# A hybrid attention, long-convolution and expert layer on one Trainium2 core: the Hyena filter network's last layer, taps, decay and transform become steps between the dense pieces

## The chip, the cores and the metric

The kernel runs on one core of a Trainium2 chip. The metric is the device time of one execution in microseconds; before the change it is 1257.59 us (median of 3 runs, 1257.53 to 1258.89).

## The reference

One layer over 256 latent tokens and 256 context tokens, width 1024, all in f32. What matters here:

```python
h = rms_norm(x, norm1_g) * (1 + sc1) + sh1          # sh1, sc1: silu(c) @ ada_w + ada_b
q, k, v, hy, gates = split(h @ w_in + b_in)         # the same for the context rows (k, v used)
oa = diff_out(diff_attention(rope(norm(q)), [k_ctx, rope(k)], [v_ctx, v], lam))
# Hyena branch
hdn = sin(freq * (z @ w1 + b1)); hdn = sin(freq * (hdn @ w2 + b2)); hdn = sin(freq * (hdn @ w3 + b3))
kf  = (hdn @ w4).reshape(L, 2, 512) * exp(-t * deltas)          # taps, decay
ob  = x0 * irfft(rfft(x1 * v) * rfft([k_fwd, 0, k_bwd reversed]))
x  += g1 * ((sig(ga) * (oa @ w_up_a) + sig(gb) * (ob @ w_up_b)) @ w_out)
x  += g2 * moe(modulated rms_norm(x))               # top 4 of 32 experts, clamped SwiGLU
```

The filter network depends on no token: it works on a fixed table of positions (33 x 256) and on its weights.

## The kernel before

**Dense pieces.** The projections are done as 128-row pieces of weight, 512 columns each, in a fixed order: q (first half, pieces 0 to 3), h1 (4 to 7), q again (8 to 11), h1 again (12 to 15), k (16 to 23), v (24 to 31), then hv, h0, the gates and the up projections. h1, hv and h0 are the three Hyena streams. Each weight and each activation is split into a rounded part and a remainder ("hi" and "lo"), and `mm3` does three multiplies with them. A weight's hi part is a ScalarE cast and its lo part a subtract on VectorE or GpSimd (`prep_hi`, `prep_lo`; a list of pieces says whose lo goes to GpSimd); the tile of two pieces is called `wsp`, and three of them rotate.

**Order.** Nothing is reordered by a scheduler: each engine executes its instructions in the order in which the code emits them, and waits where it must. After each piece `piece_done` emits the steps that the table `TASKS` lists for that piece, in the table's order; a step is a generator, and each number in its tuple is a piece after which it goes on to its next `yield`. So a step's place on an engine's queue is fixed by the table, and a step that waits holds everything behind it on that engine.

**Before the first piece** stand the loads, the statistics of x, the modulation vectors (`ada_half`, `mods_half`: the first half of channels before q, the second half between piece 7 and piece 8), the transposes of x (`columns_of`), and, woven in, all three sine layers of the filter network (`filter_layer`, `filter_sin`), the split of its last weight (`filter_weights`, two subtracts on GpSimd) and the taps (`filter_taps`, which hold four PSUM banks). The decay (`filter_decay`: two multiplies on VectorE, a sum and a difference on GpSimd, then a split into `KSD`) is a step after pieces 2 and 6, the split of the transform's matrix (`dft_parts`, subtract on GpSimd into `FG`) after piece 2. The transform (`filter_dft` and `filter_end`: 30 multiplies, tiles `ps_kf` and `ps_kn`, copied to `KF`) stands on TensorE after `mods_half(1)` and ahead of piece 8.

**Memory.** 25 slots of 8 KB per partition hold arrays and loaded weights. `ROOM` bounds the loads held at each count of takes and releases; `done` and `release` free a slot and start the next load in a fixed order (`prefetch`). The DMAs are issued by SyncE.

**Other names.** `q_out` transposes the rotated queries (`ps_qt`) after piece 22 and copies them to `QT` (a ScalarE cast, then a VectorE subtract) after piece 23. `ada` steps accumulate the rest of the modulation vectors on VectorE (`AA`). `ctx_stats`, `ctx_norm`, `ctx_columns`, `ctx_modulate` prepare the context rows (`CT`), which the k pieces need; `ps_c` are their transposes, after piece 14. The experts' weights (400 MB) stream in at the end.

Of the kernel before, what the change touches and what calls it, by code (L numbers as in the profile page):

```python
# [11 lines left out]
F32 = mybir.dt.float32  # L12
F32R = mybir.dt.float32r
# [3 lines left out]
AF = mybir.ActivationFunctionType  # L17
# [3 lines left out]
P = 128  # L21
# [12 lines left out]


TASKS = [
    ("filter_decay", (1,), (2,)), ("dft_parts", (0,), (2,)), ("filter_decay", (0,), (6,)), ("ctx_stats", (), (8,)),
    ("later_loads", (), (11,)), ("ctx_norm", (), (13,)), ("ada", (1, 0), (14,)), ("ctx_columns", (), (14, 17)),
    ("ctx_modulate", (0,), (15,)), ("ctx_modulate", (1,), (15,)), ("q_raw", (0,), (16, 18, 19)), ("ctx_modulate", (2,), (16,)),
    ("q_raw", (1,), (16, 19, 20)), ("tables", (), (16,)), ("vec2_cols", (), (17, 17)), ("hyena", (3, "h1", 4), (18, 20)),  # L40
# [116 lines left out]
def tile_kernel(ctx: ExitStack, tc: tile.TileContext, a: dict, out: bass.AP):  # L157
# [44 lines left out]
    def quarter(shape, dt=F32):  # L202
        return part("RAW", shape, dt)
# [36 lines left out]
    def want(key, shape, src):  # L240
        pending.append((key, shape, src))
# [11 lines left out]
    def then(f):  # L253
        pending.append((None, None, f))
# [17 lines left out]
    want("x", [P, 2, 1024], [(i, a["x"][0, i * P:(i + 1) * P]) for i in range(2)])  # L272
    want_half(0, 0)
    want_half(0, 1)
    then(lambda: sp.dma_start(W4[0:64], a["filt_w4"][0]))
    want_half(0, 2)
    want_half(0, 3)
    want_in("q", 0)
    q0 = w_in[0:512, 0:512].rearrange("(k p) n -> p k n", p=P)
    pending[-1] = (("in", "q", 0), [P, 4, 512], [(slice(k, k + 2), q0[:, k:k + 2]) for k in (0, 2)])  # L280
    want_in("h1", 0)
    then(lambda: filter_loads())
    for kk in range(4):
# [134 lines left out]
    def dft_parts(j):  # L418
        if j:
            FGs[1] = alloc([P, 2, 1024], "FG1", F32R)  # L420
            IDFTs.extend(FGs[1][:, j].rearrange("p (m t) -> p m t", m=4) for j in range(2))
        (gp.tensor_copy if j else act.copy)(FGs[j][:, 0], raw_fg[j])
        gp.tensor_tensor(FGs[j][:, 1], raw_fg[j], FGs[j].bitcast(F32)[:, 0], ALU.subtract)
        return iter(())

    def filter_loads():
        sp.dma_start(DEC, a["k_decay"].rearrange("(i p) c -> p i c", p=P))
        sp.dma_start(KF[:, 0:2], a["k_dft"].rearrange("(i p) c -> p i c", p=P))
# [16 lines left out]
    cT = wk.tile([P, KC, 32], F32, tag="t1", name="cT", bufs=4)  # L445
    dve.memset(cT, 0.0)
    fold = kept([P, NE], "fold")
    FS = wk.tile([P, 2, P], F32R, tag="sq", name="FS")


    B0 = kept([P, 512], "B1")
# [107 lines left out]
    def filter_layer(i):  # L559
        if i == 0:  # L560
            hs[0] = sin_layer(0, [Z[0:33, 256:320]] * 2, [Z[0:33, h * P:(h + 1) * P] for h in range(2)])
        else:
            up = [slice(64 * h, 64 * h + 64) for h in range(2)]
            hs[i] = sin_layer(i, [Z[u, 256 + 64 * i:320 + 64 * i] for u in up], [hs[i - 1][0][u] for u in up])

    def filter_sin(i):
        h, ar = hs[i]
        if i < 2:
            act.activation(h, ar, AF.Sin)
            return  # L570

        hi = wk.tile([P, P], F32R, tag="hz", name="fhi", bufs=3)
        act.activation(h, ar, AF.Sin)
        act.activation(hi, ar, AF.Sin)
        for j in range(2):
            u = slice(64 * j, 64 * j + 64)
            dve.tensor_tensor(FS[64:128, j], h[u], hi.bitcast(F32)[u], ALU.subtract)
            act.copy(FS[0:64, j], hi[u])

    def filter_weights():  # L580
        act.copy(WS[0:64, 0], W4[0:64])
        act.copy(WS[64:128, 0], W4[0:64])
# [3 lines left out]
    taps = []

    def filter_taps():
        for i in range(2):
            for d in range(2):  # L590
                ps = pst(f"ps_k{i}{d}", True)
                for j in range(2):
                    pe.matmul(ps, FS[:, i], WS[:, j, d * 512:(d + 1) * 512], start=(j == 0), stop=(j == 1))
                taps.append(ps)
        release("WS")

    def filter_decay(i):
        kw = []
        for d in range(2):
            kt = quarter([P, 512], F32)  # L600
            dve.tensor_tensor(kt, taps[2 * i + d], DEC[:, i], ALU.mult)
            unhold(f"ps_k{i}{d}")
            kw.append(kt)
        if i == 0:
            dve.memset(kw[1][0:1, :], 0.0)
        ks = quarter([P, 512], F32)
        gp.tensor_tensor(ks, kw[0], kw[1], ALU.add)
        gp.tensor_tensor(kw[1], kw[0], kw[1], ALU.subtract)
        for d, v in enumerate((ks, kw[1])):
# [12 lines left out]
    def filter_end():
        ps = pst("ps_kn")
# [111 lines left out]
    filter_weights()
    columns_of(X0, XT, "x", (0,))
    filter_sin(1)
    spin(SPINS[3])
    filter_layer(2)
    ada_half(0, 1)  # L740
    more_columns()
    ada_half(0, 2)
    columns_of(X0, XT, "x", (1,))
    done("x")
    filter_sin(2)
    prep_hi(0)
    spin(SPINS[4])
    ada_half(0, 3)
    mods_half(0)
    filter_taps()  # L750
    for k in range(4):
        modulate_split(XT, XTs, 0, dve, (k,))
        if k == 0:
# [132 lines left out]
    def filter_decays(i):
        filter_decay(i)
        return iter(())

    steps.update(dft_parts=dft_parts, filter_decay=filter_decays, later_loads=later_loads, ada=ada_step, release=release, tables=tables, lambda_=lambda_, hyena=hyena)  # L890
# [889 lines left out]
```

## Time and profile before

| | |
|---|---|
| median of 3 runs | 1257.59 us |
| the profiled execution | 1257.4 us, its span 1255.7 us |
| TensorE busy, weight loads | 88%, 42% |
| VectorE busy | 41% of the span |
| ScalarE, GpSimd busy | 22%, 13% |
| DMA | 467.10 MB, mean 372 GB/s |
| mean granted TensorE clock | 0.982 |

The times of the rows below are microseconds from the span's start; the profiled execution is 1.7 us longer than its span. An idle time in brackets says how long the engine had stood still before the instruction, and what ended it. The kernel has two parts: some 320 us up to the routing, and the experts.

### The profile page before, as it was taken

The page shows a single profiled execution, that of the slowest core. Times are in us where ns is not written, and L with a number is a line of the kernel's source. Part 1 is how long each engine was busy: PE and PEld are TensorE (multiplying, and loading weights), DVE is VectorE, ACT ScalarE, POOL GpSimd, SP SyncE. Part 2 cuts the span into 40 slices and gives each one's busy share as a digit, 9 for nine tenths or more (in the row PEclk, how much of TensorE's full clock was granted, in tenths as well). Part 3 has the DMA queues.
Part 4 walks back from the last instruction along what each step waited for, and adds up shares of the span by engine and source line. Part 5 has one row for each costly group of instructions (what it writes and reads, how often), then busy time and mean ns, then how long its engine had stood idle before and what let it go on. Part 6 is the DMA issues. An engine that isn't in the chain of part 4 may idle for free.

```text
span 1255.7 us, 14038 instructions
## 1 busy us (share of the span) xinstructions
PE 1104.1 (88%) x5547; PEld 532.6 (42%) x5547; DVE 511.1 (41%) x808; ACT 276.7 (22%) x503; POOL 168.6 (13%) x152
## 2 busy tenths in 40 slices
PE   7889789998999899897798879887988797888896
PEld 5678678897433433332242233223322332232222
DVE  5699996967222323331232223123212322223222
ACT  6563464654210111110010011001000100011110
POOL 2386455323000000000000000000000000000000
PEclk9999898999999999999999999999999999999998
DMA  9984534978899999999999999999999999999994
GB/s 335 400 313 148 175 134 191 347 293 358 334 412 417 417 417 417 418 417 418 417 416 417 417 417 417 417 417 417 418 418 418 417 417 418 417 418 417 417 416 177
DMA packets 98450, 467.10 MB, mean 372 GB/s; under 512 B 8800, under 2 KB 9804, under 8 KB 63564
## 3 DMA queue, kind: packets, MB, share of 16 engines
q1 hardware_dynamic: 95056, 462.26, 91.4%
q10 hardware_dynamic: 3324, 3.88, 1.0%
q8 instruction: 46, 0.75, 0.2%
q14 instruction: 24, 0.20, 0.0%
HBM read 465.07 MB, written 1.05 MB: 371 GB/s over the span
## 4 chain that ended last, share of the span: by engine, by line
DMA 54%; PE 28%; DVE 11%; ACT 2%; issue 2%; POOL 1%; ACTq 0%; SPq 0%; DVEq 0%; POOLq 0%
PE ps_eg L1497 6%; PE ps_eu L1497 6%; PE ps_ey L1529 5%; DMA w___w___10__3__4181<-in_exp_w_dram 2%; DMA w____w___18___0__5264<-in_exp_w_dram 2%; DMA w___w___28__7__6440<-in_exp_w_dram 2%; DMA w___w___20__3__5389<-in_exp_w_dram 2%; DMA w___w___11__7__4343<-in_exp_w_dram 2%; DMA w___w___22__3__5666<-in_exp_w_dram 2%; DMA w___w___14__3__4676<-in_exp_w_dram 2%; DMA w___w___24__3__5884<-in_exp_w_dram 2%; DMA w___w___18__3__5171<-in_exp_w_dram 2%; DMA w___w___26__3__6161<-in_exp_w_dram 2%; DMA w___w___27__7__6323<-in_exp_w_dram 2%; DMA w___w___23__7__5828<-in_exp_w_dram 2%
## 5 line engine op out<-in xcount | busy, mean ns | idle before, releaser
L1541 DVE TENSOR_TENSOR yr<-ps_ey,G 64x512 f32<-64x512 f32 x62 | 42.7, 688 | 387.2 <-PE ps_ey L1529 386.6
L479 POOL CAST pick<-both 128x128 fp32r<-128x128 f32 x32 | 24.6, 770 | 842.4 <-PE ps_eu L1380 842.3
L1542 ACT ACTIVATE YS<-yr,wsl 64x512 fp32r<-64x512 f32 x62 | 44.6, 719 | 402.9 <-DVE yr L1541 402.9
L1506 DVE TENSOR_SCALAR ga<-ps_eg 128x512 f32<-128x512 f32 x32 | 22.1, 691 | 163.4 <-PE ps_eg L1497 163.4
L1507 ACT ACTIVATE sg<-ga 128x512 f32<-128x512 f32 x32 | 20.2, 632 | 216.1 <-DVE ga L1506 216.1
L1543 DVE SCALAR_TENSOR_TENSOR YS<-yr,wsl,YS 64x512 fp32r<-64x512 f32 x62 | 46.3, 748 | 48.8 <-ACT YS L1542 48.8
L1452 PE MATMUL ps_xg<-S,XNh 128*128 128x256 f32 x128 | 37.6, 326 | 14.5 <-DVE S L1437 14.5
L1519 ACT COPY at<-ps_at 128x512 f32<-128x512 f32 x32 | 18.8, 586 | 142.6 <-PE ps_at L1517 142.6
L1627 DVE TENSOR_TENSOR X<-X,ps_sc 128x512 f32<-128x512 f32 x60 | 37.4, 680 | 3.0 <-PE ps_sc L1625 3.0
L397 PE MATMUL ps_g<-XTh,wsp 128*128 128x256 f32 x128 | 38.0, 297 | 0.0
L1452 PEld LDWEIGHTS ps_xg<-S,XNh 128*128 128x128 f32 x128 | 28.6, 223 | 19.6 <-DVE S L1437 16.9
L399 PE MATMUL ps_g<-XTh,wsp 128*128 128x256 f32 x128 | 36.5, 285 | 0.0
L398 PE MATMUL ps_g<-XTl,wsp 128*128 128x256 f32 x128 | 36.4, 285 | 0.0
L1452 PE MATMUL ps_xg<-S,XNl 128*128 128x256 f32 x128 | 36.1, 312 | 0.0
L1442 DVE TENSOR_SCALAR RAW<-ps_xg,s,sh 128x256 f32<-128x256 f32 x31 | 16.9, 544 | 35.3 <-ACT RAW L1444 35.3
L1622 PE MATMUL ps_sc<-YS,OT 128*128 128x512 f32 x120 | 30.9, 395 | 0.0
L1444 ACT ACTIVATE RAW<-ps_xg,sh,s 128x256 f32<-128x256 f32 x33 | 18.4, 564 | 49.2 <-PE ps_xg L1452 49.2
L1452 PEld LDWEIGHTS ps_xg<-S,XNl 128*128 128x128 f32 x128 | 28.7, 224 | 0.0
L397 PEld LDWEIGHTS ps_g<-XTh,wsp 128*128 128x128 f32 x128 | 24.6, 192 | 2.3 <-issue 1.8
L1622 PEld LDWEIGHTS ps_sc<-YS,OT 128*128 128x128 f32 x120 | 22.3, 188 | 7.2 <-issue 2.3
L399 PEld LDWEIGHTS ps_g<-XTh,wsp 128*128 128x128 f32 x128 | 24.7, 193 | 0.0
L398 PEld LDWEIGHTS ps_g<-XTl,wsp 128*128 128x128 f32 x128 | 24.6, 192 | 0.1
(1781 smaller groups left out, 2398.8 us busy)
## 6 DMA issues: line engine op xcount, KB each, us to landing
w_x<-in_x_dram SPq DMA_DIRECT2D x2, 512.0 KB, 4.9
w___ada___0__0__88<-in_ada_w_dram SPq DMA_DIRECT2D x2, 512.0 KB, 6.8
w___ada___0__1__91<-in_ada_w_dram SPq DMA_DIRECT2D x2, 512.0 KB, 9.5
w___ada___0__2__95<-in_ada_w_dram SPq DMA_DIRECT2D x2, 512.0 KB, 9.2
w___ada___0__3__98<-in_ada_w_dram SPq DMA_DIRECT2D x2, 512.0 KB, 12.1
w___in____q___0__101<-in_w_in_dram SPq DMA_DIRECT2D x2, 512.0 KB, 12.1
w___in____h___0__104<-in_w_in_dram SPq DMA_DIRECT2D x1, 1024.0 KB, 12.8
w___ada___1__0__108<-in_ada_w_dram SPq DMA_DIRECT2D x2, 512.0 KB, 12.1
```

Source lines behind the costliest of these rows:

```text
L397: pe.matmul(ps, ahi, bhi, start=start, stop=False, **kw)
L398: pe.matmul(ps, ahi, blo, start=False, stop=False, **kw)
L399: pe.matmul(ps, alo, bhi, start=False, stop=stop, **kw)
L479: gp.tensor_copy(pick.rearrange("p (h c) -> p h c", h=2), src.to_broadcast([P, 2, CAP]))
L1452: pe.matmul(ps[:, kk * T:(kk + 1) * T], xn[:, i, k * P:(k + 1) * P], SS[g][:, i].rearrange("p e c -> p (e c)"), start=(j == 0), stop=(j == 3))
L1497: pe.matmul(ps[64 * h:64 * h + 64, :], XG[e, k], wt[:, b * 1024 + h * 512:b * 1024 + (h + 1) * 512], start=False, stop=(k == KC - 1), skip ...
L1529: pe.matmul(yp[64 * h:64 * h + 64, :], at[:, f % 4, f // 4], wt[:, f % 2, h * 512:(h + 1) * 512], start=(f == 0), stop=(f == KC - 1))
L1541: dve.tensor_tensor(raw, yp[64 * h:64 * h + 64, :], G2[64 * h:64 * h + 64, :], ALU.mult)
L1542: act.activation(hi_[r, cs], raw, AF.Copy, scale=wsl[r, pr:pr + 1])
L1543: dve.scalar_tensor_tensor(lo_[r, cs], raw, wsl[r, pr:pr + 1], hi_.bitcast(F32)[r, cs], ALU.mult, ALU.subtract)
L1622: pe.matmul(ps, OT[pr][:, i], YP[pr][j][:, h * 512:(h + 1) * 512], start=(j == 0), stop=(j == 1 and pr > 0))
L1627: dve.tensor_tensor(xs, xs, ps, ALU.add)
```

## The change

The transposes of x come ahead of the filter's second layer. The third layer, the split of the last weight, the taps, the decay, the split of the transform's matrix and the transform itself are now steps of `TASKS`; the GpSimd instructions among them become VectorE's (the inverse transform's matrix, j = 1, stays). The filter's last weight is loaded twice, to partitions 0 to 63 and 64 to 127, behind h1's first half, and decay and transform matrix behind q's second half. `ROOM` keeps fewer loads between its counts 19 and 45, since `WS`, `FW` and the two `KSD` are held longer.

```diff
 TASKS = [
-    ("filter_decay", (1,), (2,)), ("dft_parts", (0,), (2,)), ("filter_decay", (0,), (6,)), ("ctx_stats", (), (8,)),
+    ("filter_weights", (), (3,)), ("filter", (2,), (4, 5)), ("taps", (1,), (7, 9, 10, 12)), ("dft_parts", (0,), (11,)), ("ctx_stats", (), (8,)),
+    ("taps", (0,), (11, 12, 13, 14)), ("filter_dft", (0,), (20,)), ("filter_dft", (1,), (21,)), ("filter_dft", (2,), (22,)), ("filter_dft", (3,), (23,)),
...
-    then(lambda: sp.dma_start(W4[0:64], a["filt_w4"][0]))
...
-    then(lambda: filter_loads())
+    then(lambda: [sp.dma_start(W4[64 * j:64 * j + 64], a["filt_w4"][0]) for j in range(2)])
     for kk in range(4):
         want_half(1, kk)
     want_in("q", 1)
+    then(lambda: filter_loads())
...
-        gp.tensor_tensor(FGs[j][:, 1], raw_fg[j], FGs[j].bitcast(F32)[:, 0], ALU.subtract)
+        (gp if j else dve).tensor_tensor(FGs[j][:, 1], raw_fg[j], FGs[j].bitcast(F32)[:, 0], ALU.subtract)
...
     def filter_weights():
-        act.copy(WS[0:64, 0], W4[0:64])
-        act.copy(WS[64:128, 0], W4[0:64])
-        for j in range(2):
-            gp.tensor_tensor(WS[64 * j:64 * j + 64, 1], W4[0:64], WS.bitcast(F32)[0:64, 0], ALU.subtract)
+        act.copy(WS[:, 0], W4)
+        dve.tensor_tensor(WS[:, 1], W4, WS.bitcast(F32)[:, 0], ALU.subtract)
+        return iter(())
...
+    def taps(i):
+        pss = [pst(f"ps_k{i}{d}", True) for d in range(2)]
+        for d in range(2):
+            for j in range(2):
+                pe.matmul(pss[d], FS[:, i], WS[:, j, d * 512:(d + 1) * 512], start=(j == 0), stop=(j == 1))
+        yield
...
+        yield
         ks = quarter([P, 512], F32)
-        gp.tensor_tensor(ks, kw[0], kw[1], ALU.add)
-        gp.tensor_tensor(kw[1], kw[0], kw[1], ALU.subtract)
+        dve.tensor_tensor(ks, kw[0], kw[1], ALU.add)
+        dve.tensor_tensor(kw[1], kw[0], kw[1], ALU.subtract)
...
         act.copy(KF[:, m], ps)
+        if m == 3:
+            filter_end()
+        return iter(())
...
-    for m in range(4):
-        filter_dft(m)
-    filter_end()
```

Three places show how instructions move. On TensorE, before the first piece: `ps_f` are the filter's layers, `ps_x` the transposes of x, `ps_ada` the modulation vectors. Before:

```order
L543 MATMUL ps_f_221<-fh_189,Z 64x128 x2
L532 MATMUL ps_x_238<-ident,w_x 128x128 x4
L532 MATMUL ps_x_244<-ident,w_x 128x128 x4
L487 MATMUL ps_spin_251<-ident 128x128 x8
L543 MATMUL ps_f_260<-fh_226,Z 64x128 x2
L652 MATMUL ps_ada_201<-w___ada___0__1__91,cT 32x256 x8
L514 MATMUL ps_vecb<-ident,RAW 128x24
```

and after:

```order
L533 MATMUL ps_x_220<-ident,w_x 128x128 x4
L533 MATMUL ps_x_226<-ident,w_x 128x128 x4
L659 MATMUL ps_ada_198<-w___ada___0__1__91,cT 32x256 x8
L488 MATMUL ps_spin_244<-ident 128x128 x8
L533 MATMUL ps_x_253<-ident,w_x 128x128 x4
L533 MATMUL ps_x_259<-ident,w_x 128x128 x4
L544 MATMUL ps_f_267<-fh_189,Z 64x128 x2
```

All transposes of x now stand ahead of the second layer, and the third layer is gone from here. On VectorE, from the context's statistics to the first `AA` instruction, before:

```order
L519 TENSOR_SCALAR stc<-stc 128x2
L520 RECIPROCAL stc<-stc 128x2
L375 TENSOR_TENSOR wsp_598<-w___in____h___1__281,wsp_598 128x512
L375 TENSOR_TENSOR wsp_622<-w___in____h___1__281,wsp_622 128x512
L639 TENSOR_SCALAR AA_689<-w___ada___1__0__294,col 128x1024 x2
```

and after, from the first sum of the taps on (the statistics, one `wsp` and two decay multiplies stand just ahead):

```order
L608 TENSOR_TENSOR RAW<-RAW 128x512
L609 TENSOR_TENSOR RAW<-RAW 128x512
L376 TENSOR_TENSOR wsp_550<-w___in____h___1__242,wsp_550 128x512
L424 TENSOR_TENSOR FG_78<-KF,FG_78 128x1024
L615 TENSOR_TENSOR KSD_169<-RAW,KSD_168 128x512 x2
L601 TENSOR_TENSOR RAW<-ps_k_575,FW 128x512
L601 TENSOR_TENSOR RAW<-ps_k_576,FW 128x512
L605 MEMSET RAW 1x512
L608 TENSOR_TENSOR RAW<-RAW 128x512
L609 TENSOR_TENSOR RAW<-RAW 128x512
L615 TENSOR_TENSOR KSD_169<-RAW,KSD_168 128x512 x2
L646 TENSOR_SCALAR AA_644<-w___ada___1__0__265,col 128x1024 x2
```

The whole decay of both halves and the split of `FG` now stand between the statistics and `AA`. On ScalarE, at the end of k, before (`pth` and `HX` are a Hyena stream, `ps_qt` the transposed queries):

```order
L367 CAST wsp_907<-w___in____v___0__510 128x512 x2
L873 ACTIVATE pth_936<-ps_h_422,B_130 128x256
L877 ACTIVATE HX<-pth_936,B_130 128x256
L853 CAST QT<-ps_qt_926 128x4x128
L853 CAST QT<-ps_qt_931 128x4x128
L367 CAST wsp_971<-w___in____v___1__547 128x512 x2
```

and after:

```order
L368 CAST wsp_878<-w___in____v___0__642 128x512 x2
L624 COPY KF<-ps_kf_893 128x512
L875 ACTIVATE pth_915<-ps_h_373,B_129 128x256
L879 ACTIVATE HX<-pth_915,B_129 128x256
L624 COPY KF<-ps_kf_934 128x512
L633 COPY KF<-ps_kn 1x512
L855 CAST QT<-ps_qt_905 128x4x128
L855 CAST QT<-ps_qt_910 128x4x128
L368 CAST wsp_970<-w___in____v___1__673 128x512 x2
```

The copies of the transform's last two tiles now stand ahead of the casts of the queries, because `filter_dft` stands ahead of `q_out` in `TASKS`.

## Rows read from the trace of the kernel before

**Rows 1.** The page, whole span in 40 slices: busy tenths of the DMA engines.

```profile
DMA  9984534978899999999999999999999999999994
```

**Rows 2.** Busy time by stretch; engines' busy us, granted clock, DMA share, GB/s.

```profile
core 0: us, PE busy (x) PEld busy (x) DVE busy (x) ACT busy (x) POOL busy (x), PEclk, DMA share, GB/s
70.00:80.00 10.00, 10.00 (x46) 8.24 (x45) 10.00 (x18) 7.62 (x16) 9.61 (x12) 1.00 1.04 408
120.00:130.00 10.00, 7.66 (x62) 7.04 (x61) 9.90 (x10) 2.45 (x5) 7.19 (x6) 1.00 0.63 193
```

**Rows 3.** Timeline of TensorE: start, us, instruction, idle before and its releaser.

```profile
92.02 0.63 PE L850 MATMUL ps_qt<-ident,t1q 128*128 128x128 f32 x4 [3.83 <-DVE t1q L829]
...
127.88 1.26 PE L838 MATMUL ps_kt<-ident,t1k 128*128 128x128 f32 x8 [1.47 <-DVE t1k L831]
...
132.76 1.09 PE L838 MATMUL ps_kt<-ident,t1k 128*128 128x128 f32 x4 [3.62 <-DVE KT L844]
...
155.22 2.94 PE L659 MATMUL ps_sh<-onesf,AA 128*128 128x1 f32 x13 [3.12 <-DVE AA L641]
...
187.48 0.66 PE L1047 MATMUL ps_p<-ident,PAIR 128*128 128x128 f32 x4 [3.91 <-DVE PAIR L1039]
```

**Rows 4.** Timeline from 15 to 23 us: GpSimd's and VectorE's part in the filter.

```profile
15.48 4.78 POOL L584 TENSOR_TENSOR WS<-FW,WS 64x1024 fp32r<-64x1024 f32 x2 [14.09 <-ACT WS L581]
...
18.34 2.01 DVE L548 TENSOR_SCALAR fn<-far 128x128 f32<-128x128 f32 x1
...
20.38 0.23 DVE L549 TENSOR_SCALAR fn<-fn 128x128 f32<-128x128 f32 x1
...
22.55 0.59 DVE L577 TENSOR_TENSOR FS<-fh,fhi 64x128 fp32r<-64x128 f32 x2
```

**Rows 5.** Timeline from 39 to 50 us: TensorE's waits, end of the second modulation half.

```profile
39.12 0.39 PE L399 MATMUL ps_h<-XTh,wsp 128*128 128x256 f32 x1 [2.08 <-DVE wsp L375]
...
41.90 0.39 PE L399 MATMUL ps_h<-XTh,wsp 128*128 128x256 f32 x1 [1.09 <-DVE wsp L375]
...
48.23 0.44 PE L671 MATMUL ps_adac<-ident,adarow 128*128 128x128 f32 x2 [1.28 <-DVE adarow L667]
...
49.18 0.16 DVE L677 SCALAR_TENSOR_TENSOR mods<-mods,col 128x4 f32<-128x4 f32 x1
```

**Rows 6.** Timeline of VectorE, 59 to 64 us.

```profile
59.35 0.17 DVE L519 TENSOR_SCALAR stc<-stc 128x2 f32<-128x2 f32 x1 [3.48 <-ACT PAIR L926]
...
63.37 3.47 DVE L639 TENSOR_SCALAR AA<-w___ada___1__0__294,col 128x1024 f32<-128x1024 f32 x2 [1.20 <-POOL wsp L375]
```

**Rows 7.** Timeline of VectorE: the decay's multiplies.

```profile
33.06 1.27 DVE L601 TENSOR_TENSOR RAW<-ps_k,FW 128x512 f32<-128x512 f32 x2
```

**Rows 8.** Timeline of ScalarE and TensorE: casts, context rows.

```profile
37.64 1.04 ACT L422 CAST FG<-KF 128x1024 fp32r<-128x1024 f32 x1
...
63.12 2.19 ACT L525 ACTIVATE w_ctx<-w_ctx,stc 128x1024 f32<-128x1024 f32 x2
...
65.15 1.91 PE L532 MATMUL ps_c<-ident,w_ctx 128*128 128x128 f32 x16
```

**Rows 9.** Timeline, 26 to 30 us: VectorE beside GpSimd.

```profile
26.71 2.95 POOL L375 TENSOR_TENSOR wsp<-w___in____q___0__101,wsp 128x512 fp32r<-128x512 f32 x2 [6.45 <-ACT wsp L367]
...
28.57 1.37 DVE L721 TENSOR_TENSOR XTl<-XT,XTh 128x256 fp32r<-128x256 f32 x1
30.30 0.42 DVE L721 TENSOR_TENSOR XTl<-XT,XTh 128x256 fp32r<-128x256 f32 x1
```

**Rows 10.** Timeline of the k pieces: first and 84th multiply, then the queries' casts.

```profile
68.32 0.40 PE L397 MATMUL ps_k<-wsp,XTh 128*128 128x512 f32 x1
...
87.35 0.40 PE L399 MATMUL ps_k<-wsp,CTl 128*128 128x512 f32 x1
...
92.69 0.59 ACT L853 CAST QT<-ps_qt 128x512 fp32r<-128x512 f32 x1 [3.87 <-PE ps_qt L850]
...
93.62 1.28 DVE L854 TENSOR_TENSOR QT<-ps_qt,QT 128x512 fp32r<-128x512 f32 x2
```

**Rows 11.** Busy time by stretch, as rows 2: after TensorE's wait at 92 us, and the load of the filter's last weight.

```profile
94.00:96.00 2.00, 2.00 (x6) 1.63 (x5) 1.96 (x5) 0.00 (x0) 0.00 (x0) 0.50 0.55 229
...
12.00:14.00 2.00, 1.87 (x18) 1.51 (x17) 0.61 (x2) 1.76 (x3) 0.00 (x0) 1.00 1.03 213
```

More of the change, by code (lines that the diff above doesn't have):

```diff
@@ L447, in tile_kernel @@
     fold = kept([P, NE], "fold")
-    FS = wk.tile([P, 2, P], F32R, tag="sq", name="FS")
+    FS = wk.tile([P, 2, P], F32R, tag="hz", name="FS", bufs=3)
     B0 = kept([P, 512], "B1")
@@ L580, in filter_weights, with filter_steps @@
     def filter_weights():
-        act.copy(WS[0:64, 0], W4[0:64])
-        act.copy(WS[64:128, 0], W4[0:64])
-        for j in range(2):
-            gp.tensor_tensor(WS[64 * j:64 * j + 64, 1], W4[0:64], WS.bitcast(F32)[0:64, 0], ALU.subtract)
[L586 to L597, printed above, removed]
+        act.copy(WS[:, 0], W4)
+        dve.tensor_tensor(WS[:, 1], W4, WS.bitcast(F32)[:, 0], ALU.subtract)
+        return iter(())
+    def filter_steps(i):
+        filter_layer(i)
+        yield
+        filter_sin(i)
+    def taps(i):
[4 more added lines that the diff above has]
+        yield
         kw = []
@@ L600, in filter_decay @@
             kt = quarter([P, 512], F32)
-            dve.tensor_tensor(kt, taps[2 * i + d], DEC[:, i], ALU.mult)
+            dve.tensor_tensor(kt, pss[d], DEC[:, i], ALU.mult)
             unhold(f"ps_k{i}{d}")
@@ L605, in filter_decay @@
             dve.memset(kw[1][0:1, :], 0.0)
+        yield
         ks = quarter([P, 512], F32)
-        gp.tensor_tensor(ks, kw[0], kw[1], ALU.add)
-        gp.tensor_tensor(kw[1], kw[0], kw[1], ALU.subtract)
-        for d, v in enumerate((ks, kw[1])):
+        dve.tensor_tensor(ks, kw[0], kw[1], ALU.add)
+        dve.tensor_tensor(kw[1], kw[0], kw[1], ALU.subtract)
+        sums = (ks, kw[1])
+        for d, v in enumerate(sums):
             act.copy(KSDs[0][:, d, i], v)
+        yield
+        for d, v in enumerate(sums):
             dve.tensor_tensor(KSDs[1][:, d, i], v, KSDs[0].bitcast(F32)[:, d, i], ALU.subtract)
-        if i:
-            release("FW")
+        if i == 0:
+            release("WS", "FW")
     def filter_dft(m):
@@ L725, in tile_kernel @@
     rstds(stx)
-    act.activation(warm, onesf, AF.Sin)
+    normed(X0, stx)
     filter_layer(0)
-    normed(X0, stx, (0,))
-    filter_sin(0)
-    normed(X0, stx, (1,))
     dve.tensor_copy(Z[64:128, 320:448], Z[0:64, 320:448])
@@ L733, in tile_kernel @@
     spin(SPINS[2])
-    filter_layer(1)
[L735 to L740, printed above, removed]
+    columns_of(X0, XT, "x", (0,))
+    act.activation(warm, onesf, AF.Sin)
+    filter_sin(0)
+    ada_half(0, 1)
+    spin(SPINS[3])
+    columns_of(X0, XT, "x", (1,))
+    done("x")
+    filter_layer(1)
     more_columns()
     ada_half(0, 2)
-    columns_of(X0, XT, "x", (1,))
-    done("x")
-    filter_sin(2)
+    filter_sin(1)
     prep_hi(0)
@@ L749, in tile_kernel @@
     mods_half(0)
-    filter_taps()
     for k in range(4):
@@ L885, in tile_kernel @@
     lo, hi = range(4), range(4, KC)
[L886 to L890, printed above, removed]
+    steps.update(dft_parts=dft_parts, filter_weights=filter_weights, filter=filter_steps, taps=taps, filter_dft=filter_dft, later_loads=later_loads, ada=ada_step, release=release, tables=tables, lambda_=lambda_, hyena=hyena)
     project("q", x_rows, lo)
```

10 rows, old and new, of the table ROOM are left out of this document.

## The prediction

> **What bounds the kernel now.** I read the page's slices first. The DMA digits stand at 9 from the ninth slice (about 250 us) to the end, where the experts' weights stream in [rows 1]: whatever moves the routing moves the end by as much. Before that, the stretches say who is full: VectorE is busy 10.00 of 10 us from 70 us and 9.90 of 10 from 120 us, while the DMA share falls to 0.63 [rows 2]. TensorE's timeline confirms the order: its waits between 92 and 188 us (3.83, 1.47, 3.62, 3.12, 3.91 us) all end on VectorE [rows 3]. So from about 63 us (where `AA` begins [rows 6]) the kernel is VectorE's queue, executed in order; a saving on TensorE is worth what VectorE makes of it, and whatever VectorE waits for, it passes on. Ahead of 63 us several engines share the critical path, and this is where the change works.
>
> **The change part by part.** All times below are of the profiled execution, 1257.4 us (span 1255.7 and 1.7 around it), 0.2 under the median.
>
> 1. *Ahead of the first piece.* GpSimd's two subtracts for `WS` (4.78 us) go. Beside them one `fn` instruction took 2.01 us, the same form 0.23 otherwise: 1.8 us are lost there; the two `FS` subtracts (0.59) move behind as well [rows 4]. 1.8 + 0.6 = 2.4: `mods_half(0)` comes that much earlier. Nothing else is late there, since the casts and transposes that now stand ahead are on the path already.
>
> 2. *First half of h1.* TensorE waited 2.08 and 1.09 us for a `wsp` subtract that stood behind decay and split work on VectorE, and 1.28 us for `adarow` [rows 5]. The work goes, so do 3.2 us and some 1.0 of the third. Added: four multiplies of the first taps at 0.23 (the step from one k multiply to the next: 83 of them between 68.32 and 87.35 [rows 10]) and the third layer, an estimate of 0.5: 1.4 us. Together with part 1: 2.4 + 3.2 + 1.0 − 1.4 = 5.2, so the second half of the modulation ends near 44 instead of 49.34 (49.18 + 0.16). The taps hold their PSUM banks over two to three pieces; I cost that at nothing, because each pair is released before the next is taken.
>
> 3. *VectorE up to `AA`.* Here the work that left comes back. From 49.34 the column splits and their `wsp` took until 55.87 (59.35 − 3.48 [rows 6]): 6.5 us, so now 44 + 6.5 = 50.5. Then VectorE waits for the context's statistics from ScalarE to about 51.6. Then, by the order shown, statistics 0.4; one `wsp`, two decay multiplies, two sums and one `wsp` at 0.64 each (two multiplies took 1.27 [rows 7]): 3.8, done at 55.8. It waits for ScalarE's cast of `FG` (1.04 [rows 8]) behind two casts for `KSD`: 57.1. Then `FG` 1.28, `KSD` 1.28, two multiplies 1.28, the memset (not in the trace; between 0.1 and 0.6, taken 0.5), two sums 1.28: 62.7. Beside it runs GpSimd's `wsp` work for k. In the trace one `XTl` subtract took 1.37 beside such a pair and 0.42 without: 0.95 us lost to 1.5 us of overlap [rows 9]. With one pair (2.95) beside this stretch I take 1.8, bounds 0 and 3.9: 64.5. ScalarE's casts of the sums (0.6) stand ahead of `ctx_norm`, whose first tile takes 1.1 (2.19 for two [rows 8]): the context's transposes start at 66.2 instead of 65.15, +1.0.
>
> 4. *TensorE at the columns.* VectorE's last subtract for h1 ends near 55.8, some 1.4 us later TensorE is out of work: it stands still from about 57 to 66.2, where before it had no wait at all. After a wait of 3.83 us its granted clock was 0.50 for 94 to 96 us [rows 3, 11]; that costs about 1.8 us here, bounds 0 and 3. First k multiply: 68.32 + 1.0 + 1.8 = 71.1.
>
> 5. *The k pieces, then the queries.* The first 84 multiplies take 87.35 + 0.23 − 68.32 = 19.3 us [rows 10]. Between the last pieces stand 30 multiplies of the transform, 30 × 0.23 = 6.8. With two transposes of the queries (0.9) and the last piece (2.7) `ps_kn` is done at 71.1 + 29.7 = 100.8. Taken alone, the transform would have filled the wait of 3.83 us [rows 3]; but ScalarE now executes the copy of `ps_kn` ahead of the two `QT` casts (0.59 each [rows 10]), in order. So the first `QT` subtract on VectorE can start at 100.8 + 1.2 = 102.0, and it started at 93.62 [rows 10]: +8.4. Queued behind it are a Hyena stream, `AA` and all that follows; the first v pieces wait too, since the transposed queries keep their PSUM banks until that subtract.
>
> 6. *Given back.* VectorE is full from there to the routing [rows 2], so the delay goes on. While it waits for `QT`, GpSimd runs on without hindering it; at 0.63 us (0.95 / 1.5 [rows 9]) per us of GpSimd's time beside it the standing still of 6 to 7 us gives back 0 to 4.4, and its few other waits some 0.4 more. I take 2.0.
>
> 7. *Loads and memory.* The filter's last weight, loaded into 64 partitions, went at 213 GB/s at a DMA share of 1.03, while 128 partitions had 408 at 1.04 [rows 2, 11]; loaded twice it takes about 1.6 us more, but the decay and the transform's matrix move behind: I take 0 at h1's second half, bounds 0 and 0.9. `ROOM` holds fewer loads between counts 19 and 45; VectorE's backlog covers this.
>
> Sum: +8.4 − 2.0 = +6.4, 1257.4 + 6.4 = 1263.8, so **1264 us**. Own range: part 3 contention −1.8 to +2.1, clock −1.8 to +1.2, loads to +0.9, given back 0 to 4.8 instead of 2.0: from +8.4 − 3.6 − 4.8 = 0 to +8.4 + 4.2 = +12.6; both ends at once are unlikely, about 1258 to 1269.
>
> [...]
>
> [...]
>
> **Rivals.**
>
> *The context columns do not hold TensorE: faster.* If VectorE's decay work lies in the waits of 3.48 and 1.20 us that it had there [rows 6] and the statistics come sooner, the columns start when TensorE is free, at about 57.4, the clock stays up, and the first k multiply is at 57.4 + 68.32 − 65.15 = 60.6. Then `ps_kn` ends at 90.3 and `QT` is subtracted from 91.5 on, 2.1 ahead of 93.62: about 1255.5, less if `AA` comes earlier as well. For it: the lead of 5.2 us. Against: ten VectorE instructions and the wait for `FG` now stand between. It decides if the first k multiply comes before 62.6 (93.62 − 1.2 − 29.7).
>
> *GpSimd locks VectorE out for its whole instruction.* Three subtracts of 1.3 to 1.5 us beside part 3 instead of partial slowdown: 3.9 − 1.8 = 2.1 more at the columns and at `QT`, 1266. For it: 1.37 in [rows 9]. Against: GpSimd's pair there was slow itself (2.95), so that both paid.
>
> *The late queries are absorbed: no change.* The stream that follows VectorE's `QT` is shortened by as much as it starts late, since GpSimd has emptied its queue and TensorE's waits of 3.62 and 3.12 us [rows 3] stand ready to shrink. Price: 8.4 given back, 1257.5. For it: 7.19 of 10 us of GpSimd beside VectorE at 120 us [rows 2]. Against: VectorE itself had hardly a wait there, and TensorE's waits are for it.
>
> **How the numbers follow.** Forecast 0.57, lock 0.13, absorbed 0.16, faster 0.14. A difference below 0.2% (2.5 us) can't be told from no change. Forecast and lock are slower, 0.70; absorbed is the same, 0.16; the columns' case faster, 0.14. The range of 1255 to 1270 takes in the time of each case; outside lie half of the faster one (0.07) and the ends of forecast and lock (0.06).
>
> **What would show it.** Part 1 and 2: `mods_half(1)` ends near 44, GpSimd has nothing in 15 to 25 us. Part 3: `AA` starts at 64 to 65, and the `FG` subtract follows a wait for ScalarE. Part 4: TensorE waits about 9 us ahead of `ps_c`, the clock is near 0.50 behind it, first k multiply near 71. Part 5: ScalarE's `QT` cast follows the copy of `ps_kn` at about 101.5, VectorE stands idle some 6 us ahead of the `QT` subtract. Part 6: `AA` instructions, `PAIR` and the routing come 6 us later than before. I am wrong if `ps_c` starts before 62, if the `QT` subtract starts before 96, or if VectorE has waits between 100 and 190 us that take up the delay.

## The result, and the profile after

The changed kernel takes 1267.14 us (median of 4 runs, 1266.17 to 1268.16) against 1258.24 of the kernel before beside it: a ratio of 1.0068, 95% interval 1.0054 to 1.0082, so 8.9 us slower. Timed again beside the last of the experiments it took 1266.12 (4 runs, 1264.93 to 1269.79), ratio 1.0079 (1.0056 to 1.0101). The forecast was 1264, with a range of 1255 to 1270 and 0.70 for slower. That range takes in the time of every rival, so that the measured time lies in it says little about the mechanism; the trace has to. The profiled execution took 1267.13 us, its span 1265.4, 9.7 us more than before.

I follow the trace in the order in which the prediction came. First VectorE's timeline of the changed kernel (start, us, instruction, idle before and its releaser), from the filter to the first `AA`:

```profile
18.18 0.23 DVE L549 TENSOR_SCALAR fn<-far 128x128 f32<-128x128 f32 x1
...
43.62 0.16 DVE L684 SCALAR_TENSOR_TENSOR mods<-mods,col 128x4 f32<-128x4 f32 x1
...
53.08 0.17 DVE L520 TENSOR_SCALAR stc<-stc 128x2 f32<-128x2 f32 x1 [2.79 <-ACT PAIR L921]
...
56.00 1.67 DVE L609 TENSOR_TENSOR RAW<-RAW 128x512 f32<-128x512 f32 x1
...
59.31 1.23 DVE L424 TENSOR_TENSOR FG<-KF,FG 128x1024 fp32r<-128x1024 f32 x1 [1.03 <-ACT FG L423]
60.45 2.35 DVE L615 TENSOR_TENSOR KSD<-RAW,KSD 128x512 fp32r<-128x512 f32 x2
...
65.41 0.69 DVE L609 TENSOR_TENSOR RAW<-RAW 128x512 f32<-128x512 f32 x1
66.06 1.42 DVE L615 TENSOR_TENSOR KSD<-RAW,KSD 128x512 fp32r<-128x512 f32 x2
67.39 1.41 DVE L646 TENSOR_SCALAR AA<-w___ada___1__0__265,col 128x1024 f32<-128x1024 f32 x2
```

The `fn` that took 2.01 [rows 4] takes 0.23, and the second modulation half is done at 43.78 (43.62 + 0.16) instead of 49.34 [rows 5]: a lead of 5.6 us. At the statistics it is 6.3 us (53.08 against 59.35 [rows 6]). At the first `AA` it has turned into a lag of 4.0 (67.39 against 63.37 [rows 6]): from the statistics to `AA` VectorE now takes 14.3 us instead of 4.0, because the moved instructions stand there. That much was forecast. Two things in these rows are later or longer than forecast: the statistics wait until 53.08 instead of 51.6, and one difference (1.67 against 0.69) and one pair of `KSD` subtracts (2.35 against 1.42) are stretched. ScalarE's timeline says what holds the statistics, GpSimd's what stretches the others:

```profile
49.81 1.14 ACT L368 CAST wsp<-w___in____h___1__242 128x512 fp32r<-128x512 f32 x2 [2.11 <-DMA w___in____h___1__242<-in_w_in_dram]
...
55.77 1.35 POOL L376 TENSOR_TENSOR wsp<-w___in____h___1__242,wsp 128x512 fp32r<-128x512 f32 x1 [3.44 <-ACT wsp L368]
...
60.60 3.33 POOL L376 TENSOR_TENSOR wsp<-w___in____k___0__363,wsp 128x512 fp32r<-128x512 f32 x2 [3.48 <-ACT wsp L368]
```

h1's second half lands 2.11 us after ScalarE wants it. And the stretched difference begins at 56.00, inside GpSimd's subtract (55.77 to 57.12); it ends 0.55 us after that. Of the `KSD` pair the second subtract is the stretched one: it lasts from 61.05 to 62.80, and ends 0.54 us after the first of GpSimd's two subtracts (60.60 to 62.26).

TensorE's timeline at the context's columns, and then the stretches there (busy us of each engine, granted clock, DMA share, GB/s):

```profile
67.85 3.67 PE L533 MATMUL ps_c<-ident,w_ctx 128*128 128x128 f32 x16 [8.08 <-ACT w_ctx L526]
...
73.50 0.40 PE L398 MATMUL ps_k<-wsp,XTh 128*128 128x512 f32 x1
```

```profile
66.00:68.00 2.00, 0.15 (x1) 0.15 (x2) 1.97 (x4) 1.90 (x4) 0.00 (x0) 0.50 1.08 347
68.00:70.00 2.00, 2.00 (x10) 2.00 (x11) 1.50 (x3) 2.00 (x4) 0.57 (x1) 0.50 0.83 177
...
72.00:74.00 2.00, 2.00 (x13) 1.91 (x13) 1.24 (x4) 2.00 (x5) 0.74 (x1) 0.74 0.92 316
```

TensorE stood still for 8.08 us, then ran at half clock (0.50 from 66 to 72 us) through the transposes: from the first of them to the first k multiply 73.50 − 67.85 = 5.65 us, before 68.32 − 65.15 = 3.17 [rows 8, 10]. TensorE has no wait in either stretch. In a second profile of the same kernel (after_again) the `ps_h` multiplies behind the transposes take 0.28 us from 71.21 on, where those of the first take 0.41 up to 72.60; the stretch takes 4.85 us:

```profile
67.67 3.59 PE L533 MATMUL ps_c<-ident,w_ctx 128*128 128x128 f32 x16 [8.07 <-ACT w_ctx L526]
...
72.52 0.40 PE L398 MATMUL ps_k<-wsp,XTh 128*128 128x512 f32 x1
```

Last the queries, in the timeline of ScalarE, VectorE and TensorE:

```profile
101.98 0.59 ACT L624 COPY KF<-ps_kf 128x512 f32<-128x512 f32 x1 [3.38 <-PE ps_kf L400]
103.37 0.57 ACT L633 COPY KF<-ps_kn 1x512 f32<-1x512 f32 x1 [0.80 <-PE ps_kn L400]
103.86 1.05 ACT L855 CAST QT<-ps_qt 128x512 fp32r<-128x512 f32 x2
104.46 1.29 DVE L856 TENSOR_TENSOR QT<-ps_qt,QT 128x512 fp32r<-128x512 f32 x2 [6.29 <-ACT QT L855]
105.20 0.50 PE L398 MATMUL ps_v<-wsp,XTh 128*128 128x512 f32 x1 [1.87 <-DVE QT L856]
```

The casts stand behind the copy of `ps_kn`, VectorE is idle for 6.29 us, and the subtract starts 10.84 us after that of before [rows 10]. The casts wait for the copies, and the copies (3.38 and 0.80 us idle) for the transform's last multiplies on TensorE. Of the waits of 1.47 and 3.62 us at 128 and 133 [rows 3] the first is gone in this profile and the second is 2.49, but this is no gain: VectorE, for which TensorE waited, is as late as ever, and in after_again the two waits are 1.46 and 3.62 as before.

```profile
143.61 0.63 PE L840 MATMUL ps_kt<-ident,t1k 128*128 128x128 f32 x4 [2.49 <-DVE KT L846]
...
198.64 0.65 PE L1042 MATMUL ps_p<-ident,PAIR 128*128 128x128 f32 x4 [3.43 <-DVE PAIR L1034]
```

`ps_p`, at 187.48 before [rows 3], now starts at 198.64: 11.2 us late. VectorE gave back nothing between the queries and there; in after_again the lag is 9.84 us at the subtract and 9.80 at `ps_p`. The span is only 9.7 longer because TensorE's half clock after this wait lasted longer in the profile of before, as the stretches of before and then of after show:

```profile
188.00:192.00 4.00, 3.48 (x19) 2.90 (x17) 2.18 (x3) 1.65 (x4) 3.55 (x3) 0.60 0.00 0
192.00:196.00 4.00, 3.85 (x19) 3.85 (x20) 2.65 (x5) 2.41 (x7) 0.00 (x0) 0.54 0.00 0
```

```profile
199.00:203.00 4.00, 3.92 (x20) 3.59 (x18) 2.18 (x3) 1.49 (x3) 3.71 (x3) 0.57 0.03 12
203.00:207.00 4.00, 3.69 (x30) 3.69 (x31) 2.82 (x5) 2.57 (x7) 0.00 (x0) 1.00 0.00 0
```

### The profile page after: what moved, and what is told of

It reads as the page before. It is cut to its first block, busy times and chain, and to the rows that moved or that the text cites. A ratio compares the mean times of both kernels' runs of the same rounds, so it can differ in the third digit from the quotient of the medians.

```text
span 1265.4 us, 14047 instructions
## 1 busy us (share of the span) xinstructions
PE 1113.8 (88%) x5547; PEld 541.3 (43%) x5547; DVE 512.8 (41%) x814; ACT 276.2 (22%) x502; POOL 155.9 (12%) x145
## 4 chain that ended last, share of the span: by engine, by line
DMA 52%; PE 33%; DVE 9%; ACT 2%; issue 2%; POOL 1%; ACTq 0%; SPq 0%; DVEq 0%; POOLq 0%
PE ps_eg L1492 7%; PE ps_eu L1492 6%; PE ps_ey L1524 5%; DVE AA L648 2%; DMA w___w___27__7__6322<-in_exp_w_dram 2%; DMA w___w___10__3__4180<-in_exp_w_dram 2%; PE ps_xg L1447 2%; DMA w____w___18___0__5263<-in_exp_w_dram 2%; DMA w___w___20__3__5388<-in_exp_w_dram 2%; DMA w___w___12__3__4398<-in_exp_w_dram 2%; DMA w___w___11__7__4342<-in_exp_w_dram 2%; DMA w____w___29___0__6631<-in_exp_w_dram 2%; DMA w____w___20___0__5481<-in_exp_w_dram 2%; DMA w___w___14__3__4675<-in_exp_w_dram 2%; DMA w___w___29__3__6495<-in_exp_w_dram 2%
## 5 line engine op out<-in xcount | busy, mean ns | idle before, releaser
L1447 PE MATMUL ps_xg<-S,XNh 128*128 128x256 f32 x128 | 41.6, 350 | 14.4 <-DVE S L1432 14.4
L1447 PEld LDWEIGHTS ps_xg<-S,XNh 128*128 128x128 f32 x128 | 31.7, 247 | 19.5 <-DVE S L1432 17.0
L1447 PE MATMUL ps_xg<-S,XNl 128*128 128x256 f32 x128 | 39.9, 334 | 0.0
L1447 PEld LDWEIGHTS ps_xg<-S,XNl 128*128 128x128 f32 x128 | 31.7, 248 | 0.0
L1439 ACT ACTIVATE RAW<-ps_xg,sh,s 128x256 f32<-128x256 f32 x33 | 18.5, 565 | 53.1 <-PE ps_xg L1447 53.1
```

Source lines behind the costliest of these rows:

```text
L1447: pe.matmul(ps[:, kk * T:(kk + 1) * T], xn[:, i, k * P:(k + 1) * P], SS[g][:, i].rearrange("p e c -> p (e c)"), start=(j == 0), stop=(j == 3))
```

## The experiments

Theory: the lead of 5.6 us is lost ahead of the columns, the half clock adds to it, and the queries' casts behind the transform make the largest part; VectorE passes it on. Rival: the end is set by VectorE's total work, whatever stands where.

**The last step of the transform behind the queries (q_last).**

```
-("filter_dft", (3,), (23,)),                       # ahead of q_out
 ("q_out", (0,), (22, 23)), ("q_out", (1,), (22, 23)),
+("filter_dft", (3,), (23,)),                       # behind it
```

> The changed kernel with one entry moved: the transform's last step (its 12 multiplies and the copies of ps_kf3 and ps_kn) is listed behind the queries' second step, so ScalarE's QT casts stand ahead of those copies. Theory (the queries' casts, held behind the transform, set the delay): the casts start near 98.6 instead of 103.86, VectorE's QT subtract near 99.2 instead of 104.46, and 4 to 5 us of this reach the end: 1262 to 1263. Rival (the delay is VectorE's larger amount of work, the wait before QT is slack): the subtract comes earlier but the end by less than 1 us: 1266 to 1267.

Measured 1262.48, ratio 1.0036 (1.0023 to 1.0050). In its timeline the casts stand ahead of the last two copies:

```profile
97.08 1.05 ACT L855 CAST QT<-ps_qt 128x512 fp32r<-128x512 f32 x2
...
97.68 1.29 DVE L856 TENSOR_TENSOR QT<-ps_qt,QT 128x512 fp32r<-128x512 f32 x2 [1.01 <-ACT QT L855]
...
100.56 0.59 ACT L624 COPY KF<-ps_kf 128x512 f32<-128x512 f32 x1 [2.43 <-PE ps_kf L400]
101.95 0.58 ACT L633 COPY KF<-ps_kn 1x512 f32<-1x512 f32 x1 [0.80 <-PE ps_kn L400]
```

VectorE's wait falls from 6.29 to 1.01 us and the end by some 4 us (1.0036 against 1.0068 and 1.0079). One entry of a table is worth about half of the loss: the theory holds, the rival falls.

**The clock at the columns (spin, spin_34).**

```
 def ctx_columns():
+    spin(50)        # spin_34: spin(34); multiplies of the identity
     columns_of(C, CT, "c")
```

> The changed kernel with 50 multiplies of the identity (about 7.9 us) put on TensorE ahead of the context's transposes, where it stood still for 8.08 us. Theory (the half clock after the wait is a term of its own): the clock stays at 1.00, the stretch from the first ps_c to the first k multiply takes 3.2 us as before instead of 5.65, QT comes 2.5 us earlier and the end 2 to 2.5: about 1265. Rival (VectorE's copies of the context's columns and its wsp subtract set the first k multiply, not the clock): 0 to 1 us: 1266 to 1267.

Measured 1267.21: nothing gained, but the trace shows that the test was badly sized. The 50 multiplies ended at 70.4, 2.5 us after the columns' start in the changed kernel (67.85), and so took up what the shorter stretch gave: from the first transpose to the first k multiply it is 3.18 us there (70.36 to 73.54), 2.5 less than in the changed kernel.

> The changed kernel with 34 multiplies of the identity instead of 50 ahead of the context's transposes (in the run with 50 they took 0.22 us each and lasted 2.5 us too long, which ate what the clock gave). Theory (the half clock is a term of its own): the transposes start near 67.9 as in the changed kernel, the clock is 1.00 there, the first k multiply comes 2 to 2.5 us earlier, the QT subtract near 102 and the end near 1265. Rival (VectorE's queue sets the first k multiply or takes the gain back): the end moves by less than 1 us: 1266 to 1267.

Measured 1263.94, ratio 1.0053 (1.0033 to 1.0074). Its timeline and stretch:

```profile
68.96 2.14 PE L533 MATMUL ps_c<-ident,w_ctx 128*128 128x128 f32 x16 [1.13 <-ACT w_ctx L526]
72.36 0.40 PE L398 MATMUL ps_k<-wsp,XTh 128*128 128x512 f32 x1
```

```profile
68.00:70.00 2.00, 1.04 (x8) 0.86 (x9) 2.00 (x4) 2.00 (x3) 0.00 (x0) 1.00 0.72 202
```

At full clock the same stretch takes 3.40 us instead of 5.65 and 4.85 in the two profiles of the changed kernel: 1.45 to 2.25 less. So the half clock is a term of its own. What it is worth at the end is less sure: the median is 2 to 3 lower, but the intervals of the ratios overlap, and in the profile the first k multiply comes only 0.2 to 1.1 us earlier and the `QT` subtract at 103.32 (104.46 and 103.46 without the multiplies, near 102 expected), since VectorE came to `AA` 1.1 to 1.3 us later in this execution.

**Loads (loads).**

```
     want_in("q", 1)
-    then(lambda: filter_loads())
     want("ctx", ...)
     want_in("h1", 1)
+    then(lambda: filter_loads())
```

> The changed kernel with decay and transform matrix loaded behind h1's second half instead of ahead of it and of the context. Theory (the loads ahead delay h1's second half by about 2 us, and with it the context's statistics and the whole chain to the queries): ScalarE's wait of 2.11 us for h1 goes, QT and the end come 2.1 us earlier: about 1265. Rival (the stretch is bound by VectorE's queue, which absorbs it, or the decay now comes late): 1267 to 1268.

Measured 1265.12, ratio 1.0060 (1.0037 to 1.0083). h1's load is issued at 32.91 instead of 35.77, and ScalarE no longer waits for it (its cast stands at 48.59 without a wait). The statistics come at 52.18 (53.08 and 52.90 in the two profiles of the changed kernel), although the second modulation half ends 1.0 us later in this execution, and the `QT` subtract at 102.96 instead of 104.46 and 103.46. That is 0.5 to 1.5 us in the trace, less than the 2 expected; in the end 1 to 2, inside the noise of the intervals.

**The sums back on GpSimd (pool_back).** `gp` instead of `dve` in the sum, the difference and the subtract for `FG`.

> The changed kernel with the sums and differences of the taps and the subtract of FG given back to GpSimd (the steps stay where they are). Theory (VectorE's own work ahead of AA holds the columns): VectorE loses 2.6 + 1.2 us of work, but GpSimd's two sums stand in the chain to the KSD casts and take longer than VectorE's, so that the columns come 0 to 2 us earlier and the end 0 to 2: 1265 to 1267. Rival (putting this work on VectorE is the main cost of the change): the columns come 4 us earlier or more, the end 1263 or less. Third: GpSimd's slower sums hold the columns longer: 1268 to 1270.

Measured 1268.61, ratio 1.0081 (1.0064 to 1.0097): no gain. GpSimd's part in the second half of the taps, and VectorE behind it:

```profile
65.46 1.26 POOL L608 TENSOR_TENSOR RAW<-RAW 128x512 f32<-128x512 f32 x1
66.79 1.26 POOL L609 TENSOR_TENSOR RAW<-RAW 128x512 f32<-128x512 f32 x1
67.40 1.21 DVE L615 TENSOR_TENSOR KSD<-RAW,KSD 128x512 fp32r<-128x512 f32 x1 [4.71 <-ACT KSD L612]
```

VectorE has less to do and waits 4.71 us for the longer chain instead; the columns start at 69.81. The third expectation holds at its lower end. So the change does not cost its time by giving this work to VectorE. That it costs time because the columns stand behind it is what the next run and both_ends test.

**The columns ahead of the taps on ScalarE (taps_ctx).** The entry of the second taps is listed behind `ctx_norm`, with the same pieces.

> The changed kernel with the second half of the taps listed behind ctx_norm (same pieces), so ScalarE's two KSD casts no longer stand ahead of the normalization of the context. Theory (the columns wait for ScalarE, which waits for VectorE's sums): the transposes start near 62 instead of 67.85, TensorE's wait shrinks to some 2 us and the clock stays up, but VectorE's copies of the columns still stand behind AA (68.8), so the first k multiply comes near 71 instead of 73.5 and the end 2 to 3 us earlier: 1264 to 1265. Rival (the first k multiply is held by VectorE alone): less than 1 us: 1266 to 1267.

Measured 1265.45, ratio 1.0057 (1.0040 to 1.0073), 0.7 to 1.7 us less than the changed kernel's two medians, and the intervals overlap.

```profile
61.92 1.09 PE L533 MATMUL ps_c<-ident,w_ctx 128*128 128x128 f32 x8 [2.44 <-ACT w_ctx L526]
...
70.19 0.75 PE L398 MATMUL ps_k<-wsp,XTh 128*128 128x512 f32 x1 [2.86 <-DVE CT L538]
```

The transposes start 5.9 us earlier, but the first k multiply only 3.3 and the `QT` subtract (102.85) 1.6, since VectorE copies the columns behind `AA` as before: the wait has moved to `CT`.

**The transform alone (before_dft).** The kernel before with `filter_dft` as four steps after pieces 20 to 23, `ROOM` as in the change, everything else as it was.

> One part of the change alone: the kernel before, with only the transform's four steps put between the k pieces (after pieces 20 to 23, ahead of the queries' steps), and the smaller ROOM that the longer hold of KSD needs. Theory: the first k multiply stays near 68, the 30 multiplies lie ahead of the QT casts, the QT subtract comes 5 to 6 us late (near 99) and the end 4.5 to 5.5 us: 1262 to 1264. Rival (the transform fills TensorE's wait of 3.83 us and VectorE absorbs the rest, so the loss is in taps, decay and loads): 1257 to 1259.

Measured 1260.12 (1258.33 to 1263.53 in 10 runs), ratio 1.0019 (1.0005 to 1.0032). That lies between theory and rival. What I missed: with the 6.9 us of the transform gone from ahead of piece 8, the columns come earlier. Its profile is of the slowest of its runs (1263.53), and the modulation's first half ends 4.0 us later there than before for a reason of its own (last section). If that delay is passed on whole, which no run here shows, then without it the first k multiply stands at 70.10 − 4.0 = 66.1 instead of 68.32, and the `QT` subtract at 101.07 − 4.0 = 97.1 instead of 93.62. By that reckoning the transform in k costs 3.5 us at the queries rather than the 5 to 6 expected; at the end it costs some 2.

**Both ends mended (both_ends).**

```
-("taps", (1,), (7, 9, 10, 12)), ("dft_parts", (0,), (11,)),
+("taps", (1,), (7, 7, 7, 7)),                       # decay loaded behind the last weight
-("taps", (0,), (11, 12, 13, 14)), ... ("ctx_norm", (), (13,)), ("ada", (1, 0), (14,)), ("ctx_columns", (), (14, 17)),
+("ctx_norm", (), (13,)), ("taps", (0,), (11, 12, 13, 16)), ("ctx_columns", (), (14, 17)), ("ada", (1, 0), (14,)),
+("dft_parts", (0,), (16,)),
+("filter_dft", (3,), (23,)) behind q_out; matrix loaded behind h1's second half; loads keep one slot free early on
```

> A version from what the runs showed: the changed kernel with the decay table loaded right behind the filter's last weight and the first taps all after piece 7 (in VectorE's wait of 5.6 us there), the transform's matrix loaded behind h1's second half, ctx_norm and the context's columns ahead of the second taps' sums and KSD work, AA behind the columns, FG's split after piece 16, and the transform's last step behind the queries' second step; loads keep one slot free early on. Theory (the delay came from the columns, the clock and the QT casts): the first k multiply comes near 61 to 63, the QT subtract at 91 to 94, the end level with the kernel before or 1 to 3 us under it: 1255 to 1258. Rival (VectorE's total work ahead of the routing sets the end, whatever the order): QT at 95 or later and 1260 to 1262.

Measured 1254.60 (1251.83 to 1255.80 in 7 runs), ratio 0.9971 (0.9960 to 0.9983): faster than both kernels, by 3.2 us against the kernel before beside it (1257.80) and by 11.5 to 12.5 against the changed one. VectorE's work is the same, only its order differs: the rival falls.

```profile
60.06 1.91 PE L533 MATMUL ps_c<-ident,w_ctx 128*128 128x128 f32 x16
...
63.23 0.40 PE L399 MATMUL ps_k<-wsp,XTh 128*128 128x512 f32 x1
...
90.19 0.63 PE L852 MATMUL ps_qt<-ident,t1q 128*128 128x128 f32 x4 [2.08 <-DVE t1q L831]
91.80 1.28 DVE L856 TENSOR_TENSOR QT<-ps_qt,QT 128x512 fp32r<-128x512 f32 x2
```

The transposes start without a wait, the first k multiply is 10.3 us ahead of the changed kernel's, and at the queries TensorE waits for VectorE again, as it did before.

**Its stall put back (both_ends_stall).** Only the last step of the transform ahead of `q_out` again.

> The version both_ends with only the transform's last step put back ahead of the queries' second step, as the change has it. Theory (the QT casts held behind the transform cost their whole delay, wherever the columns end): the QT subtract starts near 97.5 instead of 91.80 and the end comes 5 to 6 us later, near 1260. Rival (that cost came only from the late columns; now that TensorE waits 2.08 us for t1q the step is hidden): less than 2 us: 1255 to 1256.

Measured 1260.09, ratio 1.0015 (1.0005 to 1.0025); `after_again`, the changed kernel timed beside it, has the 1266.12 told at the start.

> The changed kernel once more, unaltered, timed beside the one above and beside the kernel before, for the size of the differences told so far. Both theories: 1266 to 1268.

```profile
63.17 0.40 PE L399 MATMUL ps_k<-wsp,XTh 128*128 128x512 f32 x1
...
90.12 0.63 PE L852 MATMUL ps_qt<-ident,t1q 128*128 128x128 f32 x4 [2.06 <-DVE t1q L831]
...
96.30 0.57 ACT L633 COPY KF<-ps_kn 1x512 f32<-1x512 f32 x1 [0.80 <-PE ps_kn L401]
96.78 1.05 ACT L855 CAST QT<-ps_qt 128x512 fp32r<-128x512 f32 x2
97.39 1.29 DVE L856 TENSOR_TENSOR QT<-ps_qt,QT 128x512 fp32r<-128x512 f32 x2 [5.58 <-ACT QT L855]
```

The subtract comes 5.6 us later (97.39 against 91.80) and the end 5.5. Early columns and TensorE's wait of 2.06 us do not hide the step: the casts cost their whole delay here too. The early columns and loads have a worth of their own: with the last step in the same place, this kernel is 6.0 us faster than the changed one beside it (1260.09 against 1266.12, intervals of the ratios apart). So the casts are about half of the loss (4 us in q_last, 5.5 here) and not clearly its largest part.

## Why the prediction was right, step by step

- *Ahead of the first piece, and h1:* right. The lead at the second modulation half is 5.6 us, forecast 5.2: 3.2 of it is there at the end of the first half (21.59 against 24.75), forecast 2.4, and 2.4 come in h1, forecast 2.8. In the runs with the same code up to there the lead varies from 3.8 (spin_34) to 5.8 (after_again), and the statistics still come at 52.3 to 53.3: a larger lead was mostly spent in ScalarE's wait for h1's load (2.17 us in after_again, none in spin_34).
- *VectorE up to the columns:* right in kind, short by 1.65 us (67.85 against 66.2). The term that was mis-sized is the loads, costed at 0 with 0.9 as its bound. No run shows the 0.9, an estimate of mine; what the trace shows is that ScalarE waited 2.11 us for h1's second half, which put the statistics at 53.08 instead of 51.6; in loads, with h1's load issued earlier, the wait is gone. The memset that the prediction calls not in the trace is there, at 43.21 us of the kernel before with 0.48 us; the 0.5 taken was right.
- *GpSimd beside it:* 1.8 was taken. The two stretched instructions lost 0.98 + 0.93 = 1.9 (1.67 − 0.69 and 2.35 − 1.42). The size is right, the reason was not, so this term came out by luck. The 0.63 per us that I read from [rows 9] is no rate: 1.37 there is the wait from 28.57 to the end of GpSimd's pair (26.71 + 2.95 = 29.66) and 0.3 more, and 1.67 here the wait to 57.12 and 0.55 more. So VectorE's instruction ended 0.3 to 0.55 us after GpSimd's each time, as by the second rival; only its price of three whole GpSimd instructions, 3.9, was too high. Two of GpSimd's three subtracts held VectorE, for 1.12 us (56.00 to 57.12) and 1.21 (61.05 to 62.26); beside the third stood the two multiplies that read PSUM, 1.27 us as without it [rows 7].
- *The clock:* right; 2.5 us in the profiled execution (5.65 − 3.17) and 1.7 in after_again (4.85 − 3.17), forecast 1.8 with 3 as its bound, and spin_34 shows it as a term of its own.
- *From the k pieces to the queries:* right. From the first k multiply to the `QT` cast 103.86 − 73.50 = 30.4 us, forecast 30.3 (29.7, and the copy of `ps_kn`); q_last and both_ends_stall show the order on ScalarE as the cause.
- *Given back:* wrong by the whole of it. The subtract was 10.84 us late and `ps_p` 11.2; none of the 2.0 came. What the span has less is the length of a half-clock stretch. The errors add up: 2.4 us too little at the queries (1.65 at the columns, 0.7 at the clock, 0.1 behind them) and 2.0 too much given back, with 0.3 more lost on the way to `ps_p`, make 4.8; the half-clock stretch of the kernel before takes 1.5 off, a matter of the two executions. That leaves the 3.3 between 1263.8 and 1267.1.
- *The rivals:* the columns did hold TensorE (8.08 us); the late queries were not absorbed. The faster case's own condition, a first k multiply before 62.6 (62.7 by its own terms), was nearly met by both_ends (63.23), and there the kernel is indeed faster, but only because the last step was moved as well: both_ends_stall nearly meets it too (63.17), and its `QT` subtract comes at 97.39 and not near 94, where that rival's 29.7 + 1.2 would put it. The rival's sum left out that TensorE still waits for `t1q` there (2.06 us): the queries are bound by VectorE, and early columns alone do not bring them.
- *A reading without weight:* the DMA digits [rows 1] are 7 and 8 in the ninth to eleventh slice and 9 only from the twelfth, about 345 us, not from 250.

Between both_ends (1254.60) and the kernel before with the transform alone (1260.12) lie 5.5 us. both_ends_stall has the early lead and the early columns of both_ends, and with the last step ahead of the queries it takes 1260.09, level with the transform alone. So all of the 5.5 us goes with the place of the last step; with the step there, lead and columns show no gain over before_dft. What stays open is what they would be worth against the kernel before with the last step in its good place, since before_dft was not run that way, and how the 6.0 us between both_ends_stall and the changed kernel divide between columns, loads and clock.

## What to carry to other kernels

When work is moved behind a piece of TensorE's program, look for what it puts in front of others on the engine that copies its result out: here two short copies ahead of the queries' casts on ScalarE, which wait for twelve multiplies, cost VectorE 5 to 6 us. Where one engine is full and executes in order, expect a stall to be passed on: here 5.6 us at the subtract were 5.5 at the end. Count nothing as given back unless a named wait shrinks. And a lead won early was kept here only where the next join (the context's columns) stood ahead of the work that was moved in.

## What the runs showed that was not expected

A VectorE instruction with one input, too, ended with GpSimd's. In before_dft's profile GpSimd's two subtracts for `WS` last from 15.01 to 19.76, and an operation of the filter's second layer on VectorE with one input, 0.23 us elsewhere, ends at 19.84:

```profile
15.01 4.75 POOL L585 TENSOR_TENSOR WS<-FW,WS 64x1024 fp32r<-64x1024 f32 x2 [13.62 <-ACT WS L582]
...
17.53 2.31 DVE L553 TENSOR_SCALAR far<-far 128x128 f32<-128x128 f32 x1
...
20.29 0.44 PE L544 MATMUL ps_f<-fh,Z 64*64 64x128 f32 x4 [4.19 <-ACT fh L570]
...
22.80 0.23 DVE L553 TENSOR_SCALAR far<-far 128x128 f32<-128x128 f32 x1
...
28.61 0.16 DVE L681 SCALAR_TENSOR_TENSOR mods<-mods,col 128x4 f32<-128x4 f32 x1
```

Three instructions ahead of it took 3.09 us, 0.94 elsewhere. So this one execution lost 4.2 us where the kernel before lost 1.8 [rows 4]. TensorE stood still for 4.19 us meanwhile, and behind that two groups of 16 `ps_ada` multiplies took 1.91 and 1.75 us instead of 1.07. Together, 2.4 and 1.5, this is the lag of 4.0 us: the first modulation half ends at 28.77 instead of 24.75. The same two subtracts thus cost 4.2 us in one execution and 1.8 in the other: this may be part of the spread of the kernel before (1255.27 to 1260.88 in the 17 runs beside q_last), which no run here tests.

Also the half clock after a wait of 3.4 to 3.9 us lasted through 188 to 196 us in one execution (0.60, 0.54) and was gone by 203 in another (0.57, then 1.00). From that `ps_p` to the next are 20.0 us in the profiles of the kernel before and of q_last, and 18.5 in the ten others: 1.5 us that no line of the program explains. The stretch at the columns varies as well: 5.65 us in one profile of the changed kernel, 4.85 in the other.
